# Seven block products in place of eight, for a quarter of K in three of four block pairs

## The chip, the cores and the metric

The kernel runs on one core of a Trainium2 chip. A core has a matrix engine (TensorE, PE in the profile), three engines for elementwise work (VectorE or DVE, ScalarE or ACT, GpSimd or POOL), a queue engine (SyncE or SP) and 16 DMA engines that move data between device memory and the on-chip memory. The engines run side by side and wait for each other through semaphores. PE writes its sums into PSUM, an accumulator memory of eight banks per partition; everything else lies in SBUF, 128 partitions wide. The metric is the device time of one execution in microseconds, the median of several runs. Before the change it is 1878.81 us (three runs, 1878.52 to 1878.86).

## The reference

Two layers of a hybrid mixer, sequence 256, width 2048, all in float32. What matters here are the products with the weights at the end of each layer:

```python
y_conv = conv_branch(c_a, c_glu, c_gate, conv_w, conv_b, conv_ln_g, conv_ln_b) @ w_proj_conv
y_mla = mla_branch(q_down, kv_down, k_pe, m_gate, cos, sin,
                   q_a_g, w_uq, kv_a_g, w_ukv, q_norm_g, k_norm_g) @ w_proj_mla
y = jax.nn.sigmoid(g_conv) * y_conv + jax.nn.sigmoid(g_mla) * y_mla
return x + y @ w_out
```

`w_proj_conv` and `w_out` are 2048 x 2048. In the kernel the first of these products is the stage **pconv**, the last is **wout**. In front of them lie the input projection (glu, down, cgate, mgate, gmla, gconv), the attention with its own small projections (uq, ukv), and pmla. The convolution branch is normalised over channels, passed through silu and multiplied by a gate before pconv.

## The kernel before

**Precision.** PE multiplies float32 in a reduced form. Each operand is therefore kept as two parts: `hi`, the value rounded to that form, and `lo`, the rest. A product is three matmuls: hi x hi, lo x hi, hi x lo, summed in PSUM. The activations (`ycT`, `yT`, `hT`, `oT`) are held as hi and lo. The weights are streamed as float32 and separated on the way: `split_hi` (line 236) copies a piece on ACT (hi<-raw), `split_lo` (line 252) subtracts on DVE (lo<-raw,hi).

**Pieces, blocks, slots.** A weight matrix is cut into blocks of 512 output columns and each block into pieces of 256 rows of K (`KS` = 2 times 128), 512 KB each. A block of pconv or wout has eight pieces. A slot (`slot_of`, line 339) works one piece: 2 row tiles of the sequence (`T`, index t) x 2 chunks of K x 3 parts = 12 matmuls of 512 columns, into two PSUM tiles (acc, one for each t). The two block sets of acc are used in turn (`banks`, line 337). `slots_of_layer` (line 105) gives the order: in pconv and wout blocks 0 and 1 alternate, two slots each; blocks 2 and 3 follow one after the other.

**Looking ahead.** Pieces are numbered in the order in which slots use them. At slot i the program issues hi for the pieces up to i+3 (four buffers) and lo up to i+2 (three buffers); each `split_hi(i)` also issues the loads up to four pieces farther (`LOAD_AHEAD`, line 225) into five raw buffers (`raw_p`, line 190). Loads go onto SP's queue in order; a load waits there until its raw buffer is free, that is until the lo of the piece five before is made.

**Order.** The order on each engine is that of the program: every instruction passes through `InOrder` (its line 171 is the one that the profile gives for nearly all of them) and is issued in order. Side work is put into slots by hand: `at_slot(n, f)` (line 265) runs f at the end of the issue of a later slot, `background` (line 294) runs what is due, and a list `fill` holds the taps of the convolution and the layer norm, which DVE does where the program's own bookkeeping thinks it idle.

**Evacuation.** After a block's last slot `evac` reads both PSUM tiles. `pconv_evac` (line 1167) multiplies by the gate, adds the attention branch, and hands the result to `four` (line 1085); `wout_evac` (line 1181) adds the residual x, which `wout_begin` (line 1176) has loaded, and in layer 0 writes it to device memory and turns it into the input of layer 1 (hT). Turning a 128 x 512 tile (`turn`, line 395) means: four small DMAs out (`park`), after four slots one back (`fetch`), after eight slots a transpose of 32 x 32 blocks on DVE, and hi and lo after it. All park and fetch DMAs are issued by POOL, in order.

**Memory.** The pool `uv` (line 193) has nine buffers, which the convolution uses for its inputs (u_t) and results (v_t, the list `vs`); `work2`, tag qk, has two, used in the attention.

Of the kernel before, what the change touches and what calls it, by code (L numbers as in the profile page):

```python
# [70 lines left out]
REVOLUTION_PIECES = 6  # L71


def revolution_pieces():
# [30 lines left out]
def slots_of_layer(layer):  # L105

    order, out, b = order_of_layer(), [], 0
    slots = [STREAM_K[s] // KS for _, _, s in order]
    while b < len(order):
        kind, i, _ = order[b]  # L110
        if (kind in ("pconv", "wout", "glu")) and i == 0:
# [23 lines left out]
def trunk(ctx: ExitStack, tc: tile.TileContext, xT, x, x_first, pos, win, wuq, wukv, wpc, wpm, wo, cst, rows, invf, out):  # L135
# [53 lines left out]
    layer_c = pool("layer_c", 1)  # L189
    raw_p = pool("raw", 5)  # L190
    split_p = pool("split", 3)
# [16 lines left out]
    streams = {"win": win, "wuq": wuq, "wukv": wukv, "wpc": wpc, "wpm": wpm, "wo": wo}  # L208
    pieces, plans = [], []
    for l in range(DEPTH):  # L210
        at, todo, blks = {}, blocks_of_layer(), []
        for kind, i, s in order_of_layer():
            n = todo[s].pop(0)
            blks.append(SimpleNamespace(kind=kind, i=i, stream=s, n=n, nk=STREAM_K[s], at=at.get(s, 0), mine={}))
            at[s] = at.get(s, 0) + STREAM_K[s] * P * n
        for b, j in slots_of_layer(l):
            blk = blks[b]
            size = P * KS * blk.n
            ap = streams[blk.stream][l, blk.at + j * size : blk.at + (j + 1) * size]
            blk.mine[j] = len(pieces)  # L220
            pieces.append((ap.rearrange("(p k c) -> p k c", p=P, k=KS), blk.n))
        plans.append((blks, slots_of_layer(l)))

    loaded, highs, done = {}, {}, {}
    LOAD_AHEAD, HI_AHEAD, LO_AHEAD = 4, 3, 2

    def load(i):
        if i >= len(pieces) or i in loaded:
            return
        if i in x_before:  # L230
            load_x(x_before.pop(i))
        ap, n = pieces[i]
        loaded[i] = t = raw_p.tile([P, KS, n], F32, tag="raw", name=f"raw{i}")
        sp.dma_start(t, ap)

    def split_hi(i):
        if i >= len(pieces) or i in highs:
# [14 lines left out]
    def split_lo(i, k=slice(0, KS)):  # L252
        if i >= len(pieces) or done.get(i, (0, 0, 0))[2] >= k.stop:
            return
        lo = done[i][1] if i in done else split_p.tile([P, KS, pieces[i][1]], F32R, tag="lo", name=f"lo{i}")
        vec.tensor_sub(lo[:, k], loaded[i][:, k], highs[i][:, k].bitcast(F32))
        done[i] = highs[i], lo, k.stop
# [7 lines left out]
    def at_slot(ahead, f):  # L265
        steps.append((clock[0] + ahead, f))
# [69 lines left out]

    banks = [0, 1]

    def slot_of(blk, j):
        last = blk.nk // KS - 1  # L340
        if j == 0:
            blk.bank = banks.pop(0)
            blk.pts = [
                acc_p.tile([P, 512], F32, tag=f"acc{blk.bank}{t}", name=f"acc{blk.mine[0]}_{t}") for t in range(T)
            ]

        def evac():
            for t in range(T):
                blk.evacuate(t, blk.pts[t][:, : blk.n])

        i, n = blk.mine[j], blk.n
        for e in ("vec", "act"):
            now[e] = max(now[e], now["pe"])
        for a in range(HI_AHEAD + 1):
            split_hi(i + a)
            if a <= LO_AHEAD:
                split_lo(i + a)
        hi, lo, _ = done[i]
        if blk.before:
            blk.before(j)  # L360
        for t, kk, part in order_of_products(i, j == last):
# [3 lines left out]
            pe.matmul(  # L365
                blk.pts[t][:, :n], stationary, w[:, kk, :],
                start=k == 0 and part == 0, stop=k == blk.nk - 1 and part == 2,
            )
        if j == last:
            banks.append(blk.bank)  # L370
            steps.insert(0, (clock[0] + 1 + blk.evac_at, evac))
        background()
# [196 lines left out]
    for l in range(DEPTH):  # L569
# [390 lines left out]
        def layernorm(vs=vs, s1=s1, C=C, keep=keep):  # L960
# [112 lines left out]
            for c in range(4):  # L1073
# [6 lines left out]
                for b in (4 + 2 * c, 5 + 2 * c) if c < 2 else ():  # L1080
                    then(apply, b)

        def four(evac_src, dst_hi, dst_lo, c, t):

# [3 lines left out]
            def use(z):  # L1090
                act.copy(hi, z)
                at_slot(1, lambda: vec.tensor_sub(lo, z, hi.bitcast(F32)))

            turn(evac_src, 512, None, then=use)

        def mgate_evac(c, t, ps, keep=keep, A=A):
# [48 lines left out]
        def gated(c, t, z, keep=keep, vs=vs):  # L1145
# [6 lines left out]

            def separated():
                hi, lo = keep["yc"]
                for b in (2 * c, 2 * c + 1):
# [10 lines left out]

        def pconv_evac(c, t, ps, keep=keep):
# [6 lines left out]
            four(g, *keep["y"], c, t)  # L1174

        def wout_begin(c, keep=keep, l=l):
            for t in range(T):
                keep["x", c, t] = wide_p.tile([P, 512], F32, tag="w", name="xres")
                sp.dma_start(keep["x", c, t], (x if l == 0 else x1_dram)[t, :, c * 512 : (c + 1) * 512])

# [39 lines left out]
        def of_block(blk, stat, evacuate, evac_at=EVAC_AT, before=None):  # L1220
            blk.stat, blk.evacuate, blk.evac_at, blk.before = stat, evacuate, evac_at, before

        def begin(blk):
# [35 lines left out]
            elif kind == "pconv":  # L1259
                while "yc" not in keep:  # L1260
                    run_fill()
                of_block(blk, stat_of(*keep["yc"]), lambda t, ps: pconv_evac(i, t, ps),
                         before=before_pconv if i == 0 else None)
            else:
                last = last_layer and i == 3
                of_block(blk, lambda k, t: stat_of(*keep["y"])(k, t), lambda t, ps, f=wout_evac: f(i, t, ps),
                         0 if last else EVAC_AT)

# [10 lines left out]
        for b, j in slots:  # L1279
            blk = blks[b]  # L1280
            if j == 0:
                begin(blk)
            if blk.kind == "wout" and j == blk.nk // KS - 3:
                wout_begin(blk.i)
            slot_of(blk, j)
# [117 lines left out]
```

## Time and profile before

| | |
|---|---|
| median of three runs | 1878.81 us |
| profiled execution | 1879.21 us |
| its span | 1877.4 us |
| matmuls in it | 8657 |
| bytes moved by DMA | 445.09 MB, 237 GB/s on average |
| loads on SP's queue (q1) | 359.65 MB, 58.9% of 16 engines' time |
| DMAs on POOL's queue (q0) | 83.41 MB, 13.6% |

The span runs from the first to the last instruction of the profiled execution; what lies around it is start and end. A group's row gives the line, engine and operation, what it writes and reads, its count, its busy time and the mean of one, and then the idle time of the engine ahead of it with what ended it. A row of the windows gives busy time and count of PE, its weight loads (PEld), DVE, ACT and POOL, then the granted clock of PE, the mean busy share of the 16 DMA engines and the rate. [...]

### The profile page before, as it was taken

Reading aid. Unit: us, or ns where it says so; the run is one execution under the profiler, and the core shown is the slowest. Engines: PE = TensorE matmul, PEld = TensorE weight load, DVE = VectorE, ACT = ScalarE, POOL = GpSimd, SP = SyncE. Lnnn points to the kernel's source line nnn. Section 1 sums busy time; section 2 is a strip of 40 time slices with the busy share of each in tenths; the row PEclk is TensorE's granted clock in tenths of the full one; section 3 lists DMA queues with packets and bytes.
Section 4 is the critical chain, followed back from the end, with each engine's and each line's share of the span. In section 5 each row is a group of like instructions: output and inputs, shape, how many; then the busy total and the mean of one; then the engine's idle time right before and its main releaser. Section 6 shows DMA issues by size and latency. Waiting matters only on the chain.

```text
span 1877.4 us, 27945 instructions
## 1 busy us (share of the span) xinstructions
PE 1872.1 (100%) x8657; PEld 1583.4 (84%) x8657; DVE 1612.0 (86%) x2964; ACT 1379.2 (73%) x2486; POOL 409.9 (22%) x762
## 2 busy tenths in 40 slices
PE   9999999999999999999999999999999999999999
PEld 8988888888888888888899888888888888888887
DVE  7999999999999987676668999999999999775764
ACT  7778888888899856544557888888887988574442
POOL 0142534332200000031421334343322000000310
PEclk9999999999999999999999999999999999999999
DMA  8786887887765666677977778788877656666775
GB/s 317 225 263 231 262 267 253 262 261 236 246 214 191 205 205 206 201 246 254 310 235 223 250 234 284 249 256 266 271 230 238 207 192 204 211 202 201 259 247 168
DMA packets 137909, 445.09 MB, mean 237 GB/s; under 512 B 23712, under 2 KB 27296, under 8 KB 137760
## 3 DMA queue, kind: packets, MB, share of 16 engines
q1 hardware_dynamic: 104256, 359.65, 58.9%
q0 software_dynamic: 33216, 83.41, 13.6%
q8 instruction: 68, 1.11, 0.3%
q14 instruction: 81, 0.66, 0.1%
q10 hardware_dynamic: 288, 0.26, 0.0%
HBM read 399.18 MB, written 44.04 MB: 236 GB/s over the span
## 4 chain that ended last, share of the span: by engine, by line
PE 100%; DVE 0%; DVEq 0%; issue 0%
PE acc L171 97%; PE s L171 2%; PE o_ps L171 1%; PE warm L171 0%; DVE zeros L171 0%; PE mean L171 0%; PE var L171 0%; DVE xres L171 0%; DVEq L1399 0%
## 5 line engine op out<-in xcount | busy, mean ns | idle before, releaser
L171 DVE TENSOR_TENSOR lo<-raw,hi 128x1024 fp32r<-128x1024 f32 (+3 forms) x687 | 811.4, 1184 | 217.5 <-PE acc L171 158.8
L171 ACT CAST hi<-raw 128x1024 fp32r<-128x1024 f32 (+3 forms) x687 | 699.7, 1022 | 399.4 <-PE acc L171 346.6
L171 PE MATMUL acc<-hi,hT 128*128 128x512 f32 (+2 forms) x1728 | 419.8, 382 | 0.0
L171 PEld LDWEIGHTS acc<-hi,hT 128*128 128x128 f32 x1728 | 319.7, 188 | 59.1
L171 ACT ACTIVATE tap<-u_t,cst 128x256 f32<-128x256 f32 x696 | 301.0, 500 | 16.1 <-DVE v_t L171 12.1
L171 PE MATMUL acc<-hi,h_hi 128*128 128x512 f32 (+2 forms) x864 | 261.5, 383 | 0.0
L171 PE MATMUL acc<-hi,h_lo 128*128 128x512 f32 (+2 forms) x864 | 260.9, 383 | 0.0
L171 DVE TENSOR_TENSOR v_t<-v_t,tap 128x256 f32<-128x256 f32 x696 | 250.9, 417 | 0.4
L171 PE MATMUL acc<-lo,h_hi 128*128 128x512 f32 (+2 forms) x864 | 229.5, 382 | 0.0
L171 PE MATMUL acc<-lo,hT 128*128 128x512 f32 (+2 forms) x864 | 229.3, 382 | 0.0
L171 PEld LDWEIGHTS acc<-hi,h_lo 128*128 128x128 f32 x864 | 161.4, 188 | 30.2
L171 PEld LDWEIGHTS acc<-lo,h_hi 128*128 128x128 f32 x864 | 160.6, 188 | 30.1
L171 PEld LDWEIGHTS acc<-lo,hT 128*128 128x128 f32 x864 | 160.6, 188 | 30.0
L171 PEld LDWEIGHTS acc<-hi,h_hi 128*128 128x128 f32 x864 | 160.5, 188 | 29.6 <-ACT hi L171 0.7
L171 POOL DMA_DIRECT2D turn_d<-gate x192 | 104.6, 553 | 326.7 <-DVE gate L171 258.3
L171 POOL DMA_DIRECT2D turned<-turn_d x88 | 49.0, 557 | 516.7 <-DVE v_t L171 282.2
L171 PE MATMUL acc<-hi,yT 128*128 128x512 f32 x512 | 127.8, 389 | 0.0
L171 PE MATMUL acc<-hi,ycT 128*128 128x512 f32 x512 | 127.7, 389 | 0.0
L171 PE MATMUL acc<-hi,oT 128*128 128x512 f32 x512 | 127.7, 389 | 0.0
L171 PE MATMUL acc<-hi,qkc 128*128 128x512 f32 (+1 forms) x512 | 118.6, 363 | 0.0
L171 DVE SCALAR_TENSOR_TENSOR v_t<-u_t,cst,v_t 128x256 f32<-128x256 f32 x264 | 113.8, 477 | 0.0
L171 PEld LDWEIGHTS acc<-hi,yT 128*128 128x128 f32 x512 | 96.1, 188 | 20.0
(168 smaller groups left out, 2157.4 us busy)
## 6 DMA issues: line engine op xcount, KB each, us to landing
raw<-in_win SPq DMA_DIRECT2D x382, 512.0 KB, 4.3
raw<-in_wpm SPq DMA_DIRECT2D x64, 512.0 KB, 3.3
raw<-in_wpc SPq DMA_DIRECT2D x64, 512.0 KB, 4.3
raw<-in_wo SPq DMA_DIRECT2D x64, 512.0 KB, 4.3
raw<-in_wukv SPq DMA_DIRECT2D x32, 512.0 KB, 4.0
turned<-turn_d POOLq DMA_DIRECT2D x56, 256.0 KB, 5.4
raw<-in_win SPq DMA_DIRECT2D x32, 384.0 KB, 4.0
raw<-in_wuq SPq DMA_DIRECT2D x32, 384.0 KB, 3.6
```

Of the source, the lines that this page charges most:

```text
L171: ins = getattr(self.engine, name)(*a, **k)
```

## The change

Write the first quarter of K of a block pair as a product of 2 x 2 blocks: two row tiles of the sequence (t = 0, 1) by two pieces of K on the side of the activations, two pieces of K (k = 0, 1) by two output blocks (e = 0, 1) on the side of the weights. That takes eight block products. Winograd's form of Strassen's scheme computes it with seven, of sums of the blocks: the sums S1 to S4 of the activations, and T1 to T4 of the weights. The change does so for pconv 2/3, wout 0/1 and wout 2/3 (`SEVEN`), in both layers. In each of these pairs the four slots (0,0), (0,1), (1,0), (1,1) are replaced by four slots a, b, c (two products of six matmuls each) and d (one product), which alternate with slots (0,2), (0,3), (0,4).

**Weights.** Where a slot used a piece, it now uses an item; the seven products take seven items: T3 and 11, T2 and 21, T4 and T1, 22. Three are plain pieces; four are sums, which are not computed on an engine but by loads: the first term is loaded into the raw buffer by SP, and each further term added by a DMA of POOL with `accum_op` (`add`): T1 = w00 + w10, T3 = w11 + w10, T2 = w00 + T3, T4 = w01 + T2 (in wek, e is the block, k the piece). The further term is a piece in device memory, or the raw buffer of another item. The adds are issued up to eight items ahead of use. Each item is separated into hi and lo as before.

**Activations.** `sums_of` makes S1 to S4 on DVE and separates them. For pconv it reads the convolution's results (vs 0 and 1), through the fill list; for wout it reads copies of the first block of y (`side`), which ACT writes beside hi; the wout pairs share one set.

**Partial sums.** After some of the products ACT copies a PSUM tile into a uv buffer (`take`: P7, P1, U2, U4); DVE makes w = U4 + P7; and when a block is evacuated each of its tiles gets one of these added or subtracted (`plus`): in pconv by one more DVE operation at the evacuation, in wout by adding it to the residual tile beforehand.

**Buffers and order.** Raw buffers go from five to eight, `LOAD_AHEAD` from four to seven; the space comes from the memory in which POOL's DMA descriptors are written, which is set to 4096 bytes. The PSUM tiles of a pair are taken crosswise from the two bank sets, and the evacuations of pconv 1 and 3 and wout 1 come a slot earlier, those of pconv 3 and wout 1 with their tiles in two successive slots.

```diff
+RAWS = 8
+SEVEN = (("pconv", 2), ("wout", 0), ("wout", 2))
+SEVEN_SLOTS = [(0, "a"), (0, 2), (0, "b"), (0, 3), (0, "c"), (0, 4), (0, "d")]
+SEVEN_REST = {
+    0: [(0, 5)] + [(1, j) for j in range(2, 6)] + [(e, j) for e in range(2) for j in (6, 7)],
+    2: [(0, j) for j in range(5, 8)] + [(1, j) for j in range(2, 8)],
+}
+SEVEN_ITEMS = {"a": ("T3", "11"), "b": ("T2", "21"), "c": ("T4", "T1"), "d": ("22",)}
...
-    raw_p = pool("raw", 5)
+    raw_p = pool("raw", RAWS)
...
+                        "11": (w[0, 0],),
+                        "21": (w[0, 1],),
+                        "22": (w[1, 1],),
+                        "T1": (w[0, 0], w[1, 0]),
+                        "T2": (w[0, 0], unit.item.get("T3")),
+                        "T3": (w[1, 1], w[1, 0]),
+                        "T4": (w[0, 1], unit.item.get("T2")),
...
-    LOAD_AHEAD, HI_AHEAD, LO_AHEAD = 4, 3, 2
+    LOAD_AHEAD, HI_AHEAD, LO_AHEAD = 7, 3, 2
...
+    def add(i, n=1):
+        while i < len(items) and items[i].adds and n:
+            load(i)
+            other = items[i].adds.pop(0)
+            if isinstance(other, int):
+                add(other, 2)
+                other = loaded[other]
+            gps.dma_start(loaded[i], other, accum_op=ALU.add)
+            n -= 1
...
         load(i)
-        highs[i] = split_p.tile([P, KS, pieces[i][1]], F32R, tag="hi", name=f"hi{i}", bufs=4)
+        add(i, 2)
+        highs[i] = split_p.tile([P, KS, items[i].n], F32R, tag="hi", name=f"hi{i}", bufs=4)
...
+    def ahead(i):
         for e in ("vec", "act"):
             now[e] = max(now[e], now["pe"])
         for a in range(HI_AHEAD + 1):
             split_hi(i + a)
             if a <= LO_AHEAD:
                 split_lo(i + a)
+        for a in (5, 6, 7, 8):
+            add(i + a, 2 if a < 6 else 1)
+
+    def products(blk, t, stat, w):
+        for part in range(3):
+            for kk in range(KS):
+                sh, sl = stat(kk)
+                pe.matmul(
+                    blk.pts[t], (sh, sl, sh)[part], w[part // 2][:, kk, :],
+                    start=t not in blk.begun, stop=part == 2 and kk == KS - 1, skip_group_check=True,
+                )
+                blk.begun.add(t)
...
+        def part(name, of, t):
+            unit.part[name] = p = uv_p.tile([P, 512], F32, tag="uv", name="part")
+            act.copy(p, of.pts[t])
...
+        for name, stat, (to, t) in {
+            "a": (("T3", S(3), (b, 1)), ("11", A(0, 0), (c, 0))),
+            "b": (("T2", S(2), (c, 0)), ("21", A(KS, 0), (b, 0))),
+            "c": (("T4", A(KS, 1), (b, 1)), ("T1", S(1), (c, 0))),
+            "d": (("22", S(4), (c, 0)),),
+        }[j]:
+            products(to, t, stat, done[unit.item[name]])
+        if j == "d":
+            u = unit.part
+            w = uv_p.tile([P, 512], F32, tag="uv", name="part")
+            at_slot(3, lambda: vec.tensor_add(w, u["U4"], u["P7"]))
+            b.plus, c.plus = ((vec.tensor_add, u["P1"]), (vec.tensor_add, u["U2"])), ((vec.tensor_sub, u["U4"]), (vec.tensor_sub, w))
...
+        if blk.unit and j in (2, 3, 4):
+            if j == 2:
+                blk.unit.take("P7", blk, 1)
+            blk.unit.take({2: "P1", 3: "U2", 4: "U4"}[j], blk.unit.pair[1], 0)
+            if j == 4:
+                blk.unit.pair[1].begun.discard(0)
+        ahead(i)
...
+            def first():
+                st["s"] = s = [one().rearrange("p n (k s) -> p n k s", k=KS) for _ in range(2)]
+                vec.tensor_sub(s[0][:, 0], z[1][:, :, ts[1]], z[0][:, :, ts[1]])
+                vec.tensor_sub(s[1][:, 0], z[0][:, :, ts[0]], z[0][:, :, ts[1]])
+
+            def second():
+                s = st["s"]
+                vec.scalar_tensor_tensor(s[0][:, 1], s[0][:, 0], -1.0, z[0][:, :, ts[0]], op0=ALU.mult, op1=ALU.subtract)
+                vec.tensor_add(s[1][:, 1], z[1][:, :, ts[0]], s[0][:, 1])
+
+            def high():
+                keep["sums"] = sums = [work2.tile([P, 4, KS, P], F32R, tag="qk", name="sums") for _ in range(2)]
+                for a in range(2):
+                    act.copy(sums[0][:, 2 * a : 2 * a + 2], st["s"][a])
+                mark("sums")
...
             g = wide_p.tile([P, 512], F32, tag="w", name="gate")
-            vec.tensor_mul(g, ps, keep["sc"][:, t, blk])
+            if plus[t] is not None:
+                join, u = plus[t]
+                join(g, ps, u)
+            vec.tensor_mul(g, ps if plus[t] is None else g, keep["sc"][:, t, blk])
...
+                keep["x", c, t] = xt = wide_p.tile([P, 512], F32, tag="w", name="xres")
+                sp.dma_start(xt, (x if l == 0 else x1_dram)[t, :, c * 512 : (c + 1) * 512])
+                if blk.plus[t] is not None:
+                    at_slot(2 if last_layer and c == 3 else 3, lambda xt=xt, of=blk.plus[t]: of[0](xt, xt, of[1]))
...
-    nc = _bacc.Bacc("TRN2", target_bir_lowering=False, num_devices=1)
+    nc = _bacc.Bacc("TRN2", target_bir_lowering=False, num_devices=1, dynamic_dma_scratch_size=4096)
```

More of the change, by code (lines that the diff above doesn't have):

```diff
@@ L110, in slots_of_layer @@
         kind, i, _ = order[b]
-        if (kind in ("pconv", "wout", "glu")) and i == 0:
+        if (kind, i) in SEVEN:
+            out += [(b + e, j) for e, j in SEVEN_SLOTS + SEVEN_REST[i]]
+            b += 2
+        elif kind in ("pconv", "wout", "glu") and i == 0:
             step = 1 if kind == "glu" and layer == 0 else 2
@@ L335, in order_of_products, with accumulator @@
         return [e for t in two for p in two for e in high(t, p)] + low(0) + low(1)
[L337 to L351, printed above, removed]
+    banks = [("00", "01"), ("10", "11")]
+    def accumulator(blk, t, bank):
+        blk.pts[t] = acc_p.tile([P, 512], F32, tag=f"acc{bank}", name=f"acc{blk.kind}{blk.i}_{t}")
+    def ahead(i):
         for e in ("vec", "act"):
@@ new lines, in slot_of, with evac @@
+    def slot_of(blk, j):
+        last = blk.nk // KS - 1
+        if j == 0:
+            blk.bank = banks.pop(0)
+            blk.begun = set()
+            for t in range(T):
+                accumulator(blk, t, blk.bank[t])
+        def evac(ts=range(T)):
+            for t in ts:
+                blk.evacuate(t, blk.pts[t][:, : blk.n])
+        i, n = blk.mine[j], blk.n
+        if blk.unit and j in (2, 3, 4):
[5 more added lines that the diff above has]
+        ahead(i)
@@ L1081, in layernorm, with four @@
                     then(apply, b)
-        def four(evac_src, dst_hi, dst_lo, c, t):
+            steps_of = sums_of([vs[0][:, :, :SEQ], vs[1][:, :, :SEQ]])
+            then(steps_of[0], after=(("separated", 3),), slots=1)
+            for step in steps_of[1:-1]:
+                then(step)
+            then(steps_of[-1], after=("sums",), slots=1)
+        def four(evac_src, dst_hi, dst_lo, c, t, side=None):
             sl = (slice(None), slice(4 * c, 4 * c + 4), slice(t * P, (t + 1) * P))
@@ L1091, in use, with sums_of, low @@
                 act.copy(hi, z)
+                if side:
+                    for k in range(2):
+                        act.copy(blocks(side[k][:, :, t * P : (t + 1) * P]), z[:, KS * k : KS * k + KS])
                 at_slot(1, lambda: vec.tensor_sub(lo, z, hi.bitcast(F32)))
             turn(evac_src, 512, None, then=use)
+        def sums_of(z, keep=keep):
+            one = lambda: uv_p.tile([P, 2, SEQ], F32, tag="uv", name="side")
+            st, ts = {}, [slice(t * P, (t + 1) * P) for t in range(T)]
+            def first():
[11 more added lines that the diff above has]
+                mark("sums")
+            def low():
+                sums = keep["sums"]
+                for a in range(2):
+                    two = slice(2 * a, 2 * a + 2)
+                    vec.tensor_sub(sums[1][:, two], st["s"][a], sums[0][:, two].bitcast(F32))
+            return first, second, high, low
         def mgate_evac(c, t, ps, keep=keep, A=A):
@@ L1221, in of_block @@
             blk.stat, blk.evacuate, blk.evac_at, blk.before = stat, evacuate, evac_at, before
+            blk.unit_before = blk.kind == "pconv" and blk.i == 3 or blk.kind == "wout" and blk.i == 1
         def begin(blk):
@@ L1280, in trunk @@
             blk = blks[b]
-            if j == 0:
-                begin(blk)
+            if j in (0, "a"):
+                for each in blk.unit.pair if j == "a" else (blk,):
+                    begin(each)
             if blk.kind == "wout" and j == blk.nk // KS - 3:
-                wout_begin(blk.i)
+                wout_begin(blk)
+            if blk.kind == "pconv" and blk.i == 3 and j == 3:
+                for a, step in zip((1, 2, 2, 3), sums_of(keep["side"])):
+                    at_slot(a, step)
+            if j in SEVEN_ITEMS:
+                if blk.before:
+                    blk.before(0)
+                seven_slot(blk, j, lambda: keep["sums"])
+                continue
             slot_of(blk, j)
```

87 lines of the change are left out of this document (63 added, 24 removed).

## The prediction

> **What bounds the kernel.** I read the page first (span, busy time, chain), then the chain inside the stages that the change touches.
>
> ```profile
> span 1877.4 us, 27945 instructions
> PE 1872.1 (100%) x8657; PEld 1583.4 (84%) x8657; DVE 1612.0 (86%) x2964; ACT 1379.2 (73%) x2486; POOL 409.9 (22%) x762
> by line: PE acc L171 100.1%
> 759.95 200.19 PE acc L171 x894
> ```
>
> TensorE is busy from end to end. The last two lines are the chain of waits in the window 760 to 960 us, which holds pconv and wout of layer 0: one unbroken piece of accumulating matmuls, in which PE waits for nobody. So a matmul that goes is worth its whole duration, as long as nothing that feeds PE falls behind. The profiled execution took 1879.21 us, its span and 1.8 us around it; that is 0.40 us over the median of 1878.81, on which I put the sum.
>
> The windows show who could fall behind. Each row is one pair of output blocks, 16 slots: pconv 0/1, pconv 2/3, wout 0/1, wout 2/3 of layer 0, then the same of layer 1. The last two columns are DMA share and GB/s.
>
> ```profile
> 766.50:810.00 43.50, 43.50 (x194) 36.03 (x193) 22.08 (x21) 19.34 (x20) 2.91 (x6) 1.00 0.64 200
> 810.00:853.50 43.50, 43.50 (x194) 36.03 (x193) 29.20 (x33) 19.01 (x21) 13.53 (x25) 1.00 0.79 265
> 853.50:897.00 43.50, 43.50 (x194) 36.03 (x193) 27.90 (x31) 20.33 (x25) 9.10 (x17) 1.00 0.77 247
> 897.00:940.50 43.50, 43.50 (x194) 36.03 (x193) 28.39 (x41) 23.68 (x41) 16.23 (x30) 1.00 0.91 314
> 1700.00:1743.50 43.50, 43.50 (x194) 36.02 (x193) 22.07 (x21) 19.34 (x20) 3.05 (x6) 1.00 0.63 200
> 1743.50:1787.00 43.50, 43.50 (x194) 36.02 (x193) 29.20 (x33) 19.01 (x21) 13.37 (x25) 1.00 0.81 265
> 1787.00:1830.50 43.50, 43.50 (x193) 36.03 (x192) 28.03 (x33) 19.00 (x21) 7.65 (x14) 1.00 0.76 250
> 1830.50:1874.00 43.50, 43.02 (x190) 35.28 (x188) 20.60 (x26) 12.80 (x13) 4.28 (x8) 1.00 0.51 169
> ```
>
> DVE and ACT have a third or more of each window free, at a full clock (1.00). The DMA engines do not: in wout 2/3 of layer 0 they are at 0.91.
>
> **The gain.** In steady state one slot (one weight piece, 12 matmuls) repeats like this:
>
> ```profile
> 903.92 1.05 ACT L171 CAST hi<-raw 128x1024 fp32r<-128x1024 f32 x1 [1.67 <-PE acc L171]
> 906.64 1.05 ACT L171 CAST hi<-raw 128x1024 fp32r<-128x1024 f32 x1 [1.67 <-PE acc L171]
> ```
>
> 2.72 us per slot, so 0.2267 us per matmul (the 389 ns that the profile gives for one is its pipelined length). A unit is a quarter of K for two blocks: eight products of 6 matmuls (2 pieces of K, 3 parts), after the change seven. Six matmuls go per unit, three units a layer, two layers: 36 x 0.2267 = **8.2 us**. Four ordinary slots become a, b, c at 2.72 and d at 1.36.
>
> **What is added on DVE and ACT.** Per unit there are seven pieces to separate where there were four, so three more hi and lo; four copies of partial sums out of PSUM (takes) on ACT; one sum w and four joins on DVE. Twice per layer the sums of the stationary side are made: four operations of 256 and two of 512 columns on DVE, two copies on ACT; and pconv 0 copies two small sides.
>
> ```profile
> L171 DVE TENSOR_TENSOR lo<-raw,hi 128x1024 fp32r<-128x1024 f32 x606 | 737.3, 1220 | 193.8 <-PE acc L171 143.0 <-issue 42.5 <-ACT hi L171 1.8
> L171 ACT CAST hi<-raw 128x1024 fp32r<-128x1024 f32 x606 | 634.9, 1051 | 366.8 <-PE acc L171 319.1 <-issue 21.9 <-DVE rsq_t L171 5.1
> L171 DVE TENSOR_TENSOR gate<-gate,ym 128x512 f32<-128x512 f32 x16 | 11.1, 692 | 0.6
> L171 DVE TENSOR_TENSOR gate<-acc,sc 128x512 f32<-128x512 f32 x16 | 10.9, 683 | 0.0
> L171 ACT COPY o_sb<-o_ps 128x512 f32<-128x512 f32 x16 | 9.3, 581 | 0.0
> L171 DVE TENSOR_TENSOR su<-su 128x256 f32<-128x256 f32 x32 | 12.0, 414 | 0.0
> ```
>
> DVE per unit: 3 x 1.22 + 0.69 + 4 x 0.68 = 7.1 us, and 4 x 0.41 + 2 x 0.68 = 3.0 us for a set of sums. At most 29.2 + 10.1 = 39.3 us of the 42.1 (15.5 slots) in pconv 2/3, and 35 in the wout pairs. ACT per unit: 3 x 1.05 + 4 x 0.58 = 5.5 us, with sums and sides below 8, so 32 of 42.1 in the fullest pair. Both hide beside PE on average. The takes stand one slot ahead of the product that overwrites or continues their bank, 2.72 us for 0.58; bounds 0 and, with three of four on the path in all six units, 10.4 us. Evacuations of the same kind leave no gap in the chain above, so 0.
>
> Locally, the worst place is the transposing of wout 0/1 into h inside the next unit, layer 0:
>
> ```profile
> 913.04 1.23 DVE L171 TENSOR_TENSOR lo<-raw,hi 128x1024 fp32r<-128x1024 f32 x1 [1.50 <-PE acc L171]
> ...
> 921.35 1.29 DVE L171 STREAM_TRANSPOSE turned<-turned 128x512 f32<-128x512 f32 x2
> 922.57 1.18 DVE L171 TENSOR_TENSOR lo<-raw,hi 128x1024 fp32r<-128x1024 f32 x1
> 923.67 2.35 DVE L171 SCALAR_TENSOR_TENSOR hT<-turned,gains,hT 128x128 fp32r<-128x128 f32 x8
> 925.94 2.35 DVE L171 TENSOR_TENSOR lo<-raw,hi 128x1024 fp32r<-128x1024 f32 x2
> ```
>
> The fourth lo after 913.04 was due at 923.92 and comes at 925.94, 2.0 us late. A lo is made two slots ahead and read after 8 of 12 matmuls, so it may be 2 x 2.72 + 1.81 - 1.22 = 6.0 us late. After the change the half slot d (1.36) and w (0.69) fall there: 4.1 late, still covered. If that cover were gone, each further microsecond would be PE's.
>
> **What is added on DMA.** Per unit seven first loads in place of four, and four accumulating transfers of 512 KB on POOL's queue, two of them from one raw tile to another. Each add waits at the head of POOL's queue for its tile's load, and parks and fetches queue behind it. The 18 further loads go onto SP's queue, whose wait now is only for a free raw tile:
>
> ```profile
> SPq L171 <- DVE lo L171: 98.2, 45, 5.8
> raw<-in_wo SPq DMA_DIRECT2D x64, 512.0 KB, 4.3
> turned<-turn_d POOLq DMA_DIRECT2D x56, 256.0 KB, 5.4
> 10.00:15.00 5.00, 5.00 (x25) 4.18 (x24) 4.75 (x8) 4.89 (x9) 0.00 (x0) 1.00 1.03 416
> 20.00:25.00 5.00, 5.00 (x27) 4.49 (x26) 3.11 (x6) 2.72 (x5) 0.00 (x0) 1.00 1.00 345
> 905.00:910.00 5.00, 5.00 (x24) 4.14 (x23) 2.33 (x2) 1.69 (x2) 2.98 (x6) 1.00 0.97 318
> 910.00:915.00 5.00, 5.00 (x24) 4.14 (x23) 3.18 (x4) 1.67 (x3) 0.55 (x1) 1.00 1.00 377
> 915.00:920.00 5.00, 5.00 (x23) 4.14 (x23) 4.72 (x11) 4.15 (x10) 0.00 (x0) 1.00 0.95 347
> ```
>
> With a share near 1 the engines moved 318 to 416 GB/s; I take 360, the mean of the last two rows, the nearest in place. Three loads add 1.57 MB to a pair. The adds are issued up to eight pieces ahead, so a unit's 2.10 MB fall into the pair before it. Layer 0, over 43.5 and then 42.1 us: pconv 0/1 200 x 43.5 + 2.10 MB = 248 GB/s; pconv 2/3 11.53 + 1.57 + 2.10 = 361; wout 0/1 10.74 + 1.57 + 2.10 = 342; wout 2/3 13.66 + 1.57 = 362. If an add costs what a load costs, the stage just fits, with seven pieces of prefetch (four before) over the crests. **Cost 0**, but this is the thin place. No accumulating transfer is in the trace; nearest row, a plain load. Below 0 nothing is to be had: the deeper prefetch removes no PE wait, as there is none. Above, the end that I take is three times a load (rival C), farther than any row of this kernel reaches.
>
> [...]
>
> The smaller ring for POOL's descriptors has no row of its own: bounds 0, as POOL is busy 22%, and one landing (5.4 us) for each of the six units, 32 us; I take 0, since a fetch may land four slots, 10.9 us, after its issue.
>
> Sum: 1878.81 - 8.2 = **1870.7 us**.
>
> **Rivals.**
> A, forecast: all hidden, 1870.7 (1869.8 to 1875, the top for small stalls at the crests). Chance 0.52.
>
> [...] Seven pieces last 12.4 us inside a unit (10 pieces in 6.5 slots); less a landing of 4.3 to 6 some 7 us are cover. [...] Chance 0.17 (1874 to 1881). [...]
>
> C, the other side: accumulating is slow in itself. At three times a load, lag 21.6 us per layer, stall 14.6, twice: 1900. It outweighs the 8.2 us from a factor of 2.1 on (360 GB/s) or 2.8 (390). Against it: nothing in the trace. Chance 0.20.
>
> D, POOL's order: an add held 5 us by its load makes parks and fetches late. The fetch issued at
>
> ```profile
> 907.03 1.67 POOL L171 DMA_DIRECT2D turned<-turn_d  x3
> ```
>
> had 1.2 us to spare: its second transfer lands near 913 and DVE transposes from 914.19, by the timeline. DVE would wait 3.8 us, of which 1.9 are covered: 1.9 us at each of up to five places, 1872.6 to 1880. Chance 0.09.
>
> E, PE doesn't get shorter, because the seven products run at a slower beat than 0.2267 us: 1878.8. Weight loads are 188 ns and need not show. Chance 0.02.
>
> **Numbers.** A measurement of this kernel tells about 0.2% from no change, 3.8 us: faster is below 1875.0, slower above 1882.6. Faster: A's 0.51, B's 0.03, D's 0.02: 0.56. Same: A 0.01, B 0.12, D 0.03, E 0.01: 0.17. Slower: C 0.20, B 0.02, D 0.04, E 0.01: 0.27. Range 1869.8 to 1890, which reaches into C up to a factor of 2.5 and leaves out some 0.18.
>
> **What would show it.** Right: 8621 matmuls, a 2.72 us beat, pairs of 42.1 us in one unbroken chain, adds landing in 4 to 6 us. B or C: chain pieces broken by raw tiles in pconv 2/3 and wout 0/1, adds landing in 10 us or more, a share of 1.0 over whole pairs. D: DVE waiting for turned tiles right after POOL waited for a load. The forecast fails above all if an accumulating transfer holds the DMA engines longer than two plain ones.

## The result, and the profile after

The changed kernel takes 1911.63 us (median of 4 runs, 1909.46 to 1915.02) against 1878.84 us for the kernel before (4 runs): a ratio of 1.0177, 95% interval 1.0159 to 1.0194. It is slower by 33 us where 8 us of gain were forecast, and above the upper end of the range, 1890.

The page's first rows, for the execution that took 1909.46 us:

```profile
span 1907.7 us, 28129 instructions
PE 1876.7 (98%) x8621; PEld 1581.8 (83%) x8621; DVE 1659.4 (87%) x3036; ACT 1411.1 (74%) x2544; POOL 431.2 (23%) x786
```

The 36 matmuls are gone (8621), yet PE is busy longer than before, 1876.7 against 1872.1 us, and it is idle for 1907.7 - 1876.7 = 31.0 us, where it was 5.3. The windows say where (columns: PE, PEld, DVE, ACT, POOL busy; granted clock, DMA share, GB/s):

```profile
60.00:760.00 700.00, 700.00 (x3254) 591.29 (x3253) 657.46 (x1275) 575.03 (x1093) 160.29 (x298) 1.00 0.74 237
760.00:960.00 200.00, 182.58 (x772) 148.43 (x771) 135.58 (x164) 101.27 (x136) 52.17 (x87) 0.95 0.88 275
960.00:1690.00 730.00, 730.00 (x3429) 621.58 (x3428) 669.56 (x1298) 583.73 (x1114) 172.51 (x321) 1.00 0.75 238
1690.00:1900.00 210.00, 201.68 (x867) 164.18 (x866) 150.02 (x182) 110.17 (x132) 40.27 (x66) 0.98 0.82 258
```

The first and the third row have no gap. All of the loss lies in pconv and wout of the two layers, and there the clock too is below 1.00. Inside the first of these stretches, the chain of waits that ends with the first stall (start, duration, what):

```profile
806.06 0.86 POOL raw L183
...
814.63 0.53 POOL turn_d L183
815.16 0.00 POOLq L183
815.16 9.70 DMA raw<-in_wpc
...
824.94 1.05 ACT hi L183
...
826.04 8.06 PE accpconv L183 x24
```

Read from the bottom: PE waits for hi of an item, ACT for the DMA that adds the second term to it (this is T1 of pconv 2/3), and that DMA was issued only at 815.16, by POOL. (InOrder's line, 171 before, is 183 here.) What POOL did until then is in its timeline:

```profile
806.06 0.86 POOL L183 DMA_DIRECT2D raw<-raw  x1 [6.82 <-DVE gate L183]
806.62 4.14 POOL L183 DMA_DIRECT2D turn_d<-gate  x7
814.61 0.56 POOL L183 DMA_DIRECT2D turn_d<-gate  x1 [3.84 <-DMA turn_d<-gate]
815.16 0.97 POOL L183 DMA_DIRECT2D raw<-in_wpc  x1
815.76 3.68 POOL L183 DMA_DIRECT2D turn_d<-gate  x6
819.95 0.56 POOL L183 DMA_DIRECT2D turn_d<-gate  x1 [0.51 <-DMA turn_d<-gate]
825.15 0.55 POOL L183 DMA_DIRECT2D turn_d<-gate  x1 [4.64 <-DMA raw<-in_wpc]
```

One add (T4's, raw<-raw) and seven parks of the turning go out, eight DMAs. The ninth stands until 814.61, which is just after T4's add has landed (814.32 by the landings in the trace's records): ACT, which needs it, starts at 814.42 with "0.36 <-DMA raw<-raw" in its own timeline. (The row of 814.61 names a park as what ended the wait; the same wait in the trace of experiment 4 is put down to the add, "4.11 <-DMA raw<-raw".) Then T1's add and seven parks go out, and the next DMA stands until 825.15, when T1's add has landed (824.87). So POOL has **eight DMAs in flight** here; the ninth waits for the landing of the one eight before it, and everything behind it waits too. The trace of before has the same, and there it cost PE nothing:

```profile
893.41 0.55 POOL L171 DMA_DIRECT2D x_dram<-xres  x1 [28.16 <-DVE xres L171]
893.94 2.21 POOL L171 DMA_DIRECT2D turn_d<-xres  x4
896.15 0.57 POOL L171 DMA_DIRECT2D x_dram<-xres  x1
896.71 1.10 POOL L171 DMA_DIRECT2D turn_d<-xres  x2
898.68 1.09 POOL L171 DMA_DIRECT2D turn_d<-xres  x2 [0.87 <-DMA x_dram<-xres]
```

1 + 4 + 1 + 2 = 8, and the ninth, at 898.68, waits for the first, which lands at 898.40. The records of both traces also show what is counted: each of POOL's DMAs (740 before, 764 in the changed kernel) signals its landing on one of eight semaphores, taken strictly in turn, and none is issued before the DMA eight before it has landed. SP's DMAs (724 and 742) use another eight and are never more than eight in flight either. No run gave either queue more of them.

The adds themselves land late, by the DMA issues (KB each, median us from issue to landing):

```profile
raw<-raw POOLq DMA_DIRECT2D x12, 512.0 KB, 7.8
raw<-in_wo POOLq DMA_DIRECT2D x8, 512.0 KB, 7.8
raw<-in_wpc POOLq DMA_DIRECT2D x4, 512.0 KB, 8.7
```

Last, PE on both sides of the stall, four matmuls each:

```profile
814.11 1.10 PE L183 MATMUL accpconv<-hi,sums 128*128 128x512 f32 x4
...
826.04 2.08 PE L183 MATMUL accpconv<-hi,sums 128*128 128x512 f32 x4 [4.93 <-ACT hi L183]
```

After 4.93 us of standing still the same four take 2.08 us in place of 1.10, and the window that holds the stall has a granted clock of 0.71 and 14 matmuls:

```profile
820.00:830.00 10.00, 5.07 (x14) 3.75 (x14) 3.50 (x3) 3.93 (x5) 3.26 (x6) 0.71 0.93 296
```

So this stall costs its length and a slow stretch behind it: by the clock records of the trace one half of the full clock is granted from 824.1 to 830.9 us. Such records, of 6.8, 3.4, 10.2, 3.4 and 3.4 us, stand at five of the six stalls, where PE stood for 4.9, 1.7 + 1.7, 9.1, 2.6 and 2.7 us. At the sixth, with waits of 1.0, 1.3 and 0.55 us in this window, the clock stays at 1.00:

```profile
1820.00:1830.00 10.00, 7.00 (x28) 4.54 (x27) 6.76 (x8) 6.78 (x10) 2.77 (x5) 1.00 1.02 352
```

### The profile page after: what moved, and what is told of

Read it like the earlier page. It is cut to its first block, busy times and chain, and to the rows that moved or that the text cites. A ratio compares the mean times of both kernels' runs of the same rounds, so it can differ in the third digit from the quotient of the medians.

```text
span 1907.7 us, 28129 instructions
## 1 busy us (share of the span) xinstructions
PE 1876.7 (98%) x8621; PEld 1581.8 (83%) x8621; DVE 1659.4 (87%) x3036; ACT 1411.1 (74%) x2544; POOL 431.2 (23%) x786
## 4 chain that ended last, share of the span: by engine, by line
PE 91%; DMA 6%; DVE 1%; issue 1%; POOL 1%; ACT 0%; DVEq 0%; POOLq 0%; ACTq 0%
PE accglu L183 18%; PE acccgate L183 9%; PE accmgate L183 9%; PE accgconv L183 9%; PE accpmla L183 9%; PE accgmla L183 9%; PE accwout L183 6%; PE accdown L183 5%; PE accpconv L183 5%; PE accukv L183 5%; PE accuq L183 4%; DMA raw<-in_wo 2%; DMA raw<-in_wpc 2%; PE s L183 2%; DMA raw<-raw 1%; PE o_ps L183 1%
## 5 line engine op out<-in xcount | busy, mean ns | idle before, releaser
L183 PE MATMUL accglu<-hi,hT 128*128 128x512 f32 x512 | 128.0, 390 | 0.0
L183 PE MATMUL accpmla<-hi,oT 128*128 128x512 f32 x512 | 127.7, 389 | 0.0
L183 PE MATMUL accpconv<-hi,ycT 128*128 128x512 f32 x472 | 120.7, 395 | 0.0
L183 PEld LDWEIGHTS accpmla<-hi,oT 128*128 128x128 f32 x512 | 96.1, 188 | 19.9
L183 PE MATMUL accwout<-hi,yT 128*128 128x512 f32 x432 | 111.8, 396 | 0.5 <-DVE yT L183 0.5
L183 PEld LDWEIGHTS accglu<-hi,hT 128*128 128x128 f32 x512 | 95.8, 188 | 19.5
L183 PEld LDWEIGHTS accpconv<-hi,ycT 128*128 128x128 f32 x472 | 90.5, 192 | 19.3
L183 PEld LDWEIGHTS accwout<-hi,yT 128*128 128x128 f32 x432 | 83.0, 193 | 19.1 <-DVE yT L183 1.4
L183 PE MATMUL accglu<-hi,h_hi 128*128 128x512 f32 x256 | 79.7, 391 | 0.0
L183 PE MATMUL accglu<-hi,h_lo 128*128 128x512 f32 x256 | 79.3, 390 | 0.0
```

The lines of the kernel that those rows point to most:

```text
L183: ins = getattr(self.engine, name)(*a, **k)
```

## The experiments

Three theories. **R**, called **O** in the later runs: POOL's order; adds, parks and fetches share one queue that issues in order with a limit on what is in flight, so each holds up the others (I first took the smaller descriptor ring for the limit). **S**: an accumulating transfer is slow in itself. **W**: the further traffic alone fills the DMA engines. Where nothing else is said, a ratio is that to the kernel before, with its 95% interval. Each diff shows the main lines of its edit, not all of them.

**1. The ring alone, in the kernel before.**

```diff
-    nc = _bacc.Bacc("TRN2", target_bir_lowering=False, num_devices=1)
+    nc = _bacc.Bacc("TRN2", target_bir_lowering=False, num_devices=1, dynamic_dma_scratch_size=4096)
```

> The kernel before with nothing changed but the memory for POOL's descriptors, 4096 bytes. Theory R (with this memory POOL can have only about eight DMAs in flight; an add that takes 8 us blocks the parks behind it, and these the next add): alone it costs little, since no add is there to block it; 1878.5 to 1881. Theory S (accumulating transfers are slow in themselves) and theory W (the DMA engines lack bandwidth): 1878.8. If it costs 10 us or more, the small ring is dear without any adds.

Measured 1878.97 us, ratio 1.0000 (0.9989 to 1.0011). The small ring costs nothing where there are no adds.

**2. The adds as plain copies.** The same 24 DMAs, bytes, queue and order, only nothing is added.

```diff
-            gps.dma_start(loaded[i], other, accum_op=ALU.add)
+            gps.dma_start(loaded[i], other)
```

> The changed kernel with the twelve pairs of second terms copied by POOL over the first in place of added (accum_op left out, so the weight sums are not formed): same bytes read from memory, same order, same ring. Theory S: landing falls from 7.8 to about 5 us and the six stalls go, 1870 to 1876. Theory R: the ring frees earlier, stalls shrink to a third, 1876 to 1885. Theory W: 1900 or more.

1879.27 us, ratio 1.0000 (0.9989 to 1.0011): 32 us of the loss go when the transfers don't accumulate. That is inside R's range, above S's by 3 us, and far from W's 1900: the further bytes alone don't do it. Two of the transfers, T2's and T4's of the first unit, are issued at 798 and 803 to 806 us in both kernels. Landing in the copying kernel, by the DMA issues of two short windows:

```profile
raw<-raw POOLq DMA_DIRECT2D x1, 512.0 KB, 3.4
raw<-raw POOLq DMA_DIRECT2D x1, 512.0 KB, 3.5
```

and in the changed kernel:

```profile
raw<-raw POOLq DMA_DIRECT2D x1, 512.0 KB, 7.0
raw<-raw POOLq DMA_DIRECT2D x1, 512.0 KB, 8.3
```

Here an add lands after 2.1 to 2.4 times as long as a copy of the same tiles, but these two are not typical. T3's, the transfer before them, is issued at 788 us in both kernels and lands after 8.3 us as an add and 7.9 as a copy. Over all of them the copies land after 6.2 (raw<-raw), 6.8 (in_wo) and 6.9 us (in_wpc) in the median, the adds after 7.8, 7.8 and 8.7: 1.15 to 1.26 times as long.

What does double is the time for which their packets occupy the DMA engines. The row of POOL's queue (packets, MB, share of 16 engines' span) in the changed kernel, with copies, and without either (experiment 3):

```profile
q0 software_dynamic: 36672, 95.99, 17.0%
q0 software_dynamic: 36672, 95.99, 15.4%
q0 software_dynamic: 33216, 83.41, 13.7%
```

Times the spans of 1907.7, 1877.8 and 1869.9 us these are 324, 289 and 256 us. For the same bytes the 24 adds take 68 us of all 16 engines and the 24 copies 33: **2.1 times**. Why it is so no run here shows.

**3. No adds at all.**

```diff
-                    unit.item[name] = item(blk.n, *of)
+                    unit.item[name] = item(blk.n, of[0])
```

> The changed kernel with all 24 adding DMAs left out (each sum is its first term alone). All theories: the adds are the only cause of the stalls, so the forecast's 1870.7 (1870 to 1873). Anything above 1874 belongs to the rest of the change: the further loads, the takes, the sums on DVE.

1871.83 us, ratio 0.9963 (0.9948 to 0.9979). The first rows of the page of this run:

```profile
span 1869.9 us, 28064 instructions
PE 1864.8 (100%) x8621; PEld 1576.6 (84%) x8621; DVE 1660.2 (89%) x3036; ACT 1412.1 (76%) x2544; POOL 410.2 (22%) x762
```

All that the change adds on DVE, ACT, PSUM and SP's queue is here, and PE has no gap. The loss of the changed kernel is its adds' alone: 1911.63 - 1871.83 = 39.8 us, of which copies would cost 7.4 and the accumulating the other 32.4. By the profiled spans it is 37.8 us: 25.9 more of idle PE and 11.9 in which PE is busy longer with the same 8621 matmuls.

**4. A larger ring, in the changed kernel.** Space for it comes from two temporaries of the attention: one shares the buffers of another, one has one buffer in place of two.

```diff
-    nc = _bacc.Bacc("TRN2", target_bir_lowering=False, num_devices=1, dynamic_dma_scratch_size=4096)
+    nc = _bacc.Bacc("TRN2", target_bir_lowering=False, num_devices=1, dynamic_dma_scratch_size=7168)
```

> The changed kernel with 7168 bytes for POOL's descriptors in place of 4096 (14 DMAs in flight in place of 8, if theory R counts rightly); the space comes from two small attention tiles (sx shares the buffers of qa, qr has one buffer in place of two). Theory R: the last add of each unit (w10 onto T1) leaves 4 to 8 us earlier, stalls of 5 to 9 us shrink to 0 to 4, 1876 to 1892. Theories S and W: still 1903 to 1915.

1912.54 us, ratio 1.0180 (1.0150 to 1.0209): no change, and POOL still stands after one add and seven parks (4.11 us, until 816.91). R's first form, with 1876 to 1892, falls: with more bytes in the ring the count stays eight.

**5. Parks behind the adds.** The parks and stores of pconv 0, pconv 2 and wout 0 are issued a slot later, so that T1's add is not behind them. The diff shows pconv; wout 0 has the same.

```diff
-            turn(evac_src, 512, None, then=use)
+            go = lambda: turn(evac_src, 512, None, then=use, at=TURNED_AT - (c in (0, 2)))
+            at_slot(1, go) if c in (0, 2) else go()
```

> The changed kernel, adds and bytes unchanged; only the small DMAs of the evacuations of pconv 0, pconv 2 and wout 0 (parks, stores) are issued one slot later, so that they stand behind the unit's adds on POOL's queue. After e4, where 14 in flight by the ring's size still showed eight, theory R is now: POOL has at most eight DMAs in flight whatever the ring, and the ninth waits for the landing of the first, so an add of 8 us holds the parks and they hold the last add. R: the last add of each unit leaves some 4 us earlier, three quarters of the stalls go, 1874 to 1888. S (an add of 8 to 10 us is too long in any place): stalls stay, 1900 to 1912.

1912.97 us, ratio 1.0181 (1.0161 to 1.0202). POOL now issues T1's add early, by its timeline:

```profile
807.09 0.88 POOL L183 DMA_DIRECT2D raw<-in_wpc  x1 [0.69 <-DMA raw<-in_wpc]
```

8 us before its time in the changed kernel, and the stall at 821 is gone. But the parks and with them the fetches are late, and DVE, which has to transpose what they bring, stands, by DVE's timeline:

```profile
832.69 0.71 DVE L183 STREAM_TRANSPOSE turned<-turned 128x512 f32<-128x512 f32 x1 [5.59 <-DMA turned<-turn_d]
```

With the turning at its old due time the stall has only been handed on. R's 1874 to 1888 is missed by 25 us.

**6. The sums on GpSimd.** No accumulating DMA: GpSimd adds raw tiles. For T3 w10 gets a plain load and a raw buffer of its own; the other sums are made of tiles that are loaded anyway.

```diff
-            gps.dma_start(loaded[i], other, accum_op=ALU.add)
+            gps.tensor_add(loaded[i], loaded[i], other)
```

> The weight sums made by GpSimd's elementwise add out of raw tiles (one more plain load per unit, w10, on SP's queue) in place of the accumulating DMAs; T1 is formed as w10 plus the tile of product 11. No accumulating transfer, no 8 us landing; four adds of 128x1024 per unit on GpSimd, whose duration no trace shows: above 1.1 us (twice its memset of 128x512, 0.55 us), taken as 2 to 3. R and S both: the stalls go, 1871 to 1875; it should beat both kernels. W (bandwidth): eight first loads per unit in place of four still load the engines, 1876 or more. If GpSimd takes over 5 us for one, sums come late and PE stalls again, 1880 and more.

1903.81 us, ratio 1.0140 (1.0123 to 1.0157). An addition of 128 x 1024 takes 2.49 us in the mean, but T4's stood behind 16 parks on the same queue and ACT waited for such sums (33.6 us in six waits). Both theories had 1871 to 1875. Order on POOL again, though nothing accumulates in DMA.

**7. The turning later as well.** As experiment 5, but only pconv 0 and wout 0 are parked later, and for blocks 0 and 1 of both stages the fetch comes two slots and the transpose three slots later, counted from the parks.

```diff
-            turn(evac_src, 512, None, then=use)
+            spare = 2 * (c < 2)
+            go = lambda: turn(evac_src, 512, None, then=use, at=TURNED_AT + spare + (c < 2), fetch_at=FETCH_AT + spare)
+            at_slot(1, go) if c == 0 else go()
```

> Accumulating DMAs as in the changed kernel and, as in e5, the parks behind the adds; now the evacuations of pconv 0/1 and wout 0/1 also fetch two slots later and transpose three slots later, so that DVE doesn't stand at a tile that isn't back (the wait that e5 showed in place of the late add). Theory R (POOL's order and its eight places in flight, with adds of 8 us that fill them): most stalls go, 1876 to 1892. Theory S (an add is too long in any place): 1900 or more.

1897.82 us, ratio 1.0101 (1.0080 to 1.0121): 14 us come back by order alone, with the same adds. 26 us over experiment 3 stay, and the time lies between R's 1876 to 1892 and S's 1900. The window 850 to 890 us shows what is left in it, first without adds (experiment 3):

```profile
850.00:890.00 40.00, 40.00 (x177) 33.00 (x176) 33.50 (x39) 22.47 (x26) 5.52 (x10) 1.00 0.88 304
```

then with copies (experiment 2):

```profile
850.00:890.00 40.00, 40.00 (x178) 32.96 (x177) 33.41 (x38) 22.68 (x26) 8.78 (x16) 1.00 0.94 358
```

and with adds in the better order (this run):

```profile
850.00:890.00 40.00, 35.76 (x151) 27.46 (x150) 33.65 (x39) 22.14 (x26) 9.39 (x15) 1.00 0.99 326
```

With adds the engines are at 0.99 while they move less than with copies at 0.94. So the adds also fill the DMA engines, in a stretch that is at 0.88 without them, as their 2.1 times of engine time would have it.

**8. The sums on GpSimd, in order.** Experiment 6 with the sums of T4 and T1 ahead of the parks, and the turning as in experiment 7.

```diff
-        for a in (5, 6, 7, 8):
-            add(i + a, 2 if a < 6 else 1)
+        for a in (7, 8, 9):
+            if i + a < len(items) and items[i + a].lead == a:
+                add(i + a)
```

> e6 (sums by GpSimd's elementwise add, 2.4 us each by e6's trace) with its last two sums of each unit ordered ahead of the parks, and parks, fetches and transposes of pconv 0/1 and wout 0/1 later as in e7. In e6 the sum T4 stood behind 16 parks and ACT waited 34 us for it, six times. Theory R: all stalls go, 1871 to 1876, below both kernels. Theory W or an unseen cost of the sums: above 1880.

1904.11 us, ratio 1.0133 (1.0116 to 1.0150), no better, where 1871 to 1876 was expected. Now DVE is late. Its timeline, two rows of the evacuation of pconv 1:

```profile
804.55 0.68 DVE L183 TENSOR_TENSOR gate<-accpconv,sc 128x512 f32<-128x512 f32 x1
...
808.09 2.17 DVE L183 TENSOR_TENSOR gate<-gate,ym 128x512 f32<-128x512 f32 x1
```

and GpSimd beside it:

```profile
803.46 6.26 POOL L183 TENSOR_TENSOR raw<-raw,raw 128x1024 f32<-128x1024 f32 x2 [2.00 <-DMA raw<-in_wpc]
```

The second kind of row took 0.69 us before. Beside GpSimd's addition it takes 2.17, while the first, one of whose inputs lies in PSUM, keeps its 0.68. The evacuation's other tile in this stretch has 0.68 and 2.18. What makes the difference, no run here shows.

**9. T1's adds alone.**

```diff
-                    unit.item[name] = item(blk.n, *of)
+                    unit.item[name] = item(blk.n, *(of if name == "T1" else of[:1]))
```

> The changed kernel with one of its four adds per unit, that of T1; T2, T3 and T4 are used with their first term alone, so that part of the computation is left out. O (order and count of POOL's transfers: T1's add is late since it is issued behind T4's add, which still holds one of POOL's eight places, and behind the turning's parks): with no other add on the queue at most a stall of T1's own landing is left; PE idle under 12 us, time 1872 to 1884. S (an accumulating transfer is late by its own 8 us, wherever it stands): T1's add still lands 8 us or more after its issue and the stalls stay, PE idle near 30 us, time above 1900.

1874.46 us, ratio 0.9979 (0.9968 to 0.9990). PE is idle for 1871.9 - 1865.2 = 6.7 us. The very add at which the changed kernel stood six times costs 2.6 us over experiment 3 when the others are away, though its landing is still 6.1 us (pconv) and 7.8 us (wout) in the median. S's time above 1900 is refuted. It is what O has, that this add is late for what stands before it; but without the other 18 adds the DMA engines also have less to do, and the run does not separate the two.

**10. All but T1's.**

```diff
-                    unit.item[name] = item(blk.n, *of)
+                    unit.item[name] = item(blk.n, *(of[:1] if name == "T1" else of))
```

> The changed kernel without T1's adds (T1 is used with its first term alone, so that part of the computation is left out); those of T2, T3 and T4 stay, 18 of 24. O: the stall that stood at T1 goes, but T4's add and the turning's fetches behind it still meet the limit of eight: 1875 to 1895, with the remaining waits at DMA into turn_d or turned. S: T4's add is now the last and the stall moves to it: three quarters of the loss or more, 1900 and above. If adds were slow only in their sum of bytes, the loss would be 18/24 of 39.8 us: 1902.

1892.85 us (two runs, 1889.21 and 1896.48), ratio 1.0074 (1.0056 to 1.0092). O's range, near its upper end: 21.0 us over experiment 3 with 18 adds, 2.6 with the other six, 39.8 with all 24. The costs don't add up, which fits adds that hold up each other and the turning.

**11. The sums formed ahead of time.** From mgate on, far before pconv, POOL copies the 12 first terms of a layer to device memory and adds the 12 further ones there, one transfer every five slots. The units then use seven plain loads each.

```diff
+    def form_sums(l):
+        order = ("T3", "T1", "T2", "T4")
+        every = sorted(ahead_sums[l], key=lambda e: order.index(e[0]))
+        moves = [(d, first, {}) for _, d, first, _ in every] + [(d, other, dict(accum_op=ALU.add)) for _, d, _, other in every]
+        for k, (d, of, how) in enumerate(moves):
+            at_slot(1 + 5 * k, lambda d=d, of=of, how=how: gps.dma_start(d, of, max_dma_last_dim=1024, **how))
...
+                    if len(of) > 1:
+                        unit.sums[name] = d = dram.tile([P, KS, 512], F32, tag=f"s{l}{blk.kind}{blk.i}{name}", name="sum_dram")
+                        ahead_sums[l].append((name, d, *of))
+                        of = (d,)
```

> The changed kernel with the sums of weights formed early: from mgate 0 on, in each layer, POOL copies the 12 first terms to device memory and adds the 12 further terms there, one transfer every five slots; in pconv and wout each of the seven items is then one plain load and no add is issued. Some 31 MB of further traffic, in stages whose DMA share is 0.58 to 0.64. O and S alike: an add that has tens of microseconds to land costs nothing, so the time is that of the kernel without adds and a little more, 1871 to 1876, below both kernels. W (what counts is the traffic): stalls at raw buffers between mgate and gconv, time above 1880.

**1872.04 us** (5 runs, 1871.83 to 1872.11), ratio 0.9963 (0.9949 to 0.9977): 6.8 us faster than the kernel before, 39.6 faster than the changed one, 0.2 over experiment 3. The DMA issues and one window of it:

```profile
sum_dram<-in_wo POOLq DMA_DIRECT2D x24, 512.0 KB, 10.7
raw<-sum_dram SPq DMA_DIRECT2D x24, 512.0 KB, 4.3
sum_dram<-sum_dram POOLq DMA_DIRECT2D x12, 512.0 KB, 15.7
```

```profile
470.00:560.00 90.00, 90.00 (x401) 74.64 (x400) 87.48 (x148) 77.65 (x132) 24.10 (x38) 1.00 0.95 299
```

The 12 adds whose further term is itself one of these sums (T2's and T4's) land after 15.7 us in the median, twice as late as the adds of the changed kernel, and the engines reach a share of 0.95 there; it costs nothing, since nobody waits. The chain through pconv and wout is unbroken again:

```profile
765.87 85.87 PE accpconv L183 x378
851.74 84.69 PE accwout L183 x372
```

**12. The turning on ACT's queue.** The adds stay; from pconv on ACT issues the parks, fetches and stores of x1.

```diff
+            if blk.kind in ("pconv", "uq"):
+                turns_by[0] = act if blk.kind == "pconv" else gps
```

> The changed kernel, complete, with its 24 adds as they are; from pconv on, the turning's parks and fetches and the stores of x1 are issued by ACT instead of POOL, so that POOL's queue holds nothing but the adds (and the last layer's output stores). O (order and count of POOL's transfers): adds no longer stand behind parks, nor parks and fetches behind adds; what stays is the chain of T2's and T4's adds and some waits of ACT for the tiles that it parks: 1872 to 1890, PE idle under 15 us. S (an accumulating transfer comes too late by its own 8 us): little changes, 1900 or more, stalls at hi for want of T4 and T1.

1956.55 us, ratio 1.0405 (1.0386 to 1.0423): far from O's 1872 to 1890. S's "1900 or more" covers the number, but not its "little changes". T1's add went out at 807.69 us in place of 815.16, as O has it, by POOL's timeline:

```profile
807.69 0.87 POOL L183 DMA_DIRECT2D raw<-in_wpc  x1 [0.57 <-DVE gate L183]
```

but now ACT stands among its parks, and with it every hi and every copy out of PSUM behind them:

```profile
806.24 7.50 ACTq L183 DMA_DIRECT2D turn_d<-gate  x8
813.83 1.04 ACT L183 CAST hi<-raw 128x1024 fp32r<-128x1024 f32 x1 [9.63 <-DMA turn_d<-gate]
```

What stood in front of POOL's adds stands in front of ACT's work. The run may change one thing more: in the trace of the changed kernel the only two DMAs that ACT issues, stores of the output, signal on two of the eight semaphores of SP's loads. Whether ACT's parks and SP's loads held up each other here was not shown. Experiment 12 says that the parks must not stand ahead of what PE is about to need, on whatever queue; it doesn't tell how much POOL's adds alone would cost.

## Why the prediction was wrong

**The gain** was right in its mechanism: 8621 matmuls, and without adds the chain is unbroken. Its size was a little too large, 8.2 us against 1878.82 - 1871.83 = 7.0 in experiment 3. In experiment 11 the 62.5 slots of pconv and wout take 85.87 + 84.69 = 170.6 us, or 2.729 a slot where 2.72 was reckoned; that is 0.6 us per layer. Why the slot is longer stays open.

**DVE, ACT and the takes** at nothing: right. Experiment 3 has them all and no gap.

**The step that failed is "If an add costs what a load costs, the stage just fits ... Cost 0, but this is the thin place".** Two things are wrong in it. The size: an add lands in 7.8 to 8.7 us in the median and not in the "4 to 6", where a plain load of the same kernel takes 4.3 (in_wpc) or 6.3 (in_wo), and it occupies the DMA engines 2.1 times as long as a copy. And the price put on such a factor: the prediction reckons it as bytes over bandwidth less prefetch, and finds under C that the 8.2 us are outweighed from a factor of 2.1 on, which is a time of about 1879; the kernel with a measured 2.1 takes 1911.63, 33 us more. For rival B's range, 1874 to 1881 at a chance of 0.17, no run shows a ground; what the runs showed in its place are those 2.1 times and 1911.63 us. Even as plain copies the 24 transfers cost 7.4 us and not 0. An add is not only traffic. T4's waits for T2's, which waits for T3's, each for a whole landing (8.3, 7.0 and 8.3 us for T3's, T2's and T4's of the first unit), so that their delays add up one behind the other; and the adds take their turn on a queue in which other transfers wait for them and they for others.

**That queue is rival D**, the right place for at least the 14 us of experiment 7, with too small a price. It looked at one direction, fetches behind a held add, at 1.9 us each. The other direction was the dearer one: the last add of a unit behind 8 parks, which themselves stand because an earlier add is one of eight in flight. The row of the kernel before that shows the limit was there to be read, at 898.68 us, and the prediction took POOL's 22% of busy time for room. The bound that it wrote down for the ring, one landing for each of six units, is of the loss's size, though not from the ring (experiments 1 and 4); it was set to 0 with a reason that speaks of fetches alone. Experiment 7 gives 14 us for a better order with the same adds; experiment 5 shows a wait handed on by it at no gain, and experiments 9 and 10 fit it without separating it from the adds' traffic.

**Rival C**, three times a load for 1900, has the right sign and nearly the size. Its start is right, that accumulating costs by itself (32.4 of the 39.8 us, experiment 2); its factor of three is not the 2.1 that was measured, and its account is bytes over bandwidth alone. That its time comes near is luck.

**A term that was missing altogether** is the clock. Of the 37.8 us between the spans of the changed kernel and of experiment 3, 11.9 are PE busy with the same matmuls for longer. By the clock records of the changed kernel's trace PE was busy for 20.3 us at a granted clock of one half, which is 10.2 us lost. The rest is not the clock: in experiment 7, whose waits of PE are of 2.0 us or less, the granted clock is 0.999, a loss of about 2 us of its 1895.4, and PE is still busy for 1873.4 us, 8.6 more than in experiment 3. What makes the difference, no run here shows.

**What stays open:** how the 26 us that stay in experiment 7, and with them the 32.4 of the accumulating, divide between the adds' own landing, the DMA engines at 0.99, and POOL's limit of eight. Experiment 12 was to tell them apart and did not. More semaphores for POOL's DMAs would test the limit; no run did.

## What to carry to other kernels

Price a DMA that something waits for by its landing, by the DMAs that its queue still has in flight and by what stands before it in order, not by its bytes and the engine's busy share; look in the trace of before for how many DMAs go out in a row until one waits for a landing. A sum of constants that is needed in a tight stage can be formed long before, even slowly, and be read back with a plain load: the same adds cost 39.8 us in place and 0.2 us ahead of time. And when PE is the bound, a stall can cost more than its length: here 25.9 us of idle PE came with 11.9 of longer busy time, 10.2 of it reckoned to the half clock.

## What was not expected of the hardware

- POOL had at most eight DMAs in flight (764 DMAs in the changed kernel, 740 before), and with a ring of 7168 bytes it stood after eight again (4.11 us, experiment 4); the ninth waited for the one eight before it. They signal on eight semaphores in turn, by the records of both traces.
- For the same bytes an accumulating DMA occupied the DMA engines 2.1 times as long as a plain one (68 against 33 us for 24, the changed kernel and experiment 2 over experiment 3), while its landing was 1.15 to 1.26 times as long in the median (7.8 to 8.7 against 6.2 to 6.9 us).
- Issuing an accumulating DMA held POOL for 0.86 to 1.24 us (all 24 in the changed kernel), a plain one of the same size for 0.54 to 0.57 (the 12 of layer 0 in experiment 2).
- After a stall of 4.9 us four matmuls took 2.08 us instead of 1.10, and the granted clock of that 10 us window was 0.71; in another such window waits of 1.0, 1.3 and 0.55 us left it at 1.00.
- A DVE operation of 128 x 512 with both inputs in SBUF (gate<-gate,ym) went from 0.69 to 2.17 us beside an addition on GpSimd (experiment 8); one with an input in PSUM kept its 0.68.
- Issuing eight parks took ACT 7.50 us (experiment 12); seven took POOL 4.14 us in the changed kernel.
